# Rotation tables in one round, the opening's squares off GpSimd, the first norm ahead of block 1's split, history copies on ScalarE

## The chip, the cores and the metric

The kernel runs on one core of one Trainium2 chip. The metric is the device time of one execution in microseconds (us), the median over several runs. A core has TensorE (PE in the profile; its weight loads are PEld), VectorE (DVE), ScalarE (ACT), GpSimd (POOL) and SyncE (SP, which issues nearly all transfers here; its queue is SPq). Matmul results land in PSUM, everything else is in SBUF or in device memory (HBM).

## The reference

One hybrid decoder layer over 2048 tokens of width 1024, in float32. Cut to what matters:

```python
h = rms_norm(x, norm_in)
c_q, c_kv, k_rope, gdn_qkv, gdn_a, gdn_b, mem_q, gate = split_cols(h @ w_in, ...)
cos, sin = cos(positions * inv_freq), sin(positions * inv_freq)      # 32 frequencies
q = rms_norm(c_q) @ w_q_b;  kv = rms_norm(c_kv) @ w_kv_b             # q_rope, k_rope rotated
o_mla = causal_mla(q_nope, q_rope, k_nope, k_rope, v)                # 4 heads
qkv = silu(causal_depthwise_conv(gdn_qkv, gdn_conv))                 # 4 taps
o_gdn = rms_norm(gated_delta_rule_chunked(...))                      # 4 heads
o_mem = memory_attention(mem_q, mk, mv)                              # 4 heads, 256 memory tokens
x = x + (concat(o_mla, o_gdn, o_mem) * silu(gate)) @ w_out
y = rms_norm(x, norm_final)
```

## The kernel before

All large products are done as three matmuls of halves: an operand is split into a rounded high part and the rest (`hh` and `hl` for the activations, `wh` and `wl` for the weights), and `mm3` (line 317) adds high x high, high x low and low x high into one PSUM buffer. The tokens are worked in two halves of 1024 (`hf`), each of two blocks of 512 (`b`).

A planner runs while the program is written. It keeps a clock for every engine (`T`, line 146), charges each instruction a cost (`act_cost`, `dve_cost`, `pool_cost`, `pe_cost`, from line 204), and resumes background generators (`bg`, `spawn`, `pump`, lines 322 to 338) when the clock of PE passes their due time. It also decides by these clocks where a weight's low half is computed (`lesser`, line 618: GpSimd if its clock isn't ahead of PE's by more than a slack, otherwise VectorE). The order of writing is a priority; the framework's scheduler then orders each engine's instructions, save those that are pinned (`pin`, line 236) and keep the order in which they were written. Each engine works its queue in order.

The opening (`x_opening`, line 1911) is pinned. It loads four weight tiles and eight tiles of x^T for block 0, splits both, and runs four projections on block 0. x is not yet normed: the split takes the gain `norm_in` only (`x_split`, line 582), and the norm's factor is applied when a PSUM buffer is emptied (`scaled`, line 567, by `R[b]`). `prepare` (line 1939) splits one x tile, squares it on ScalarE and adds the square to `accs[b]`, on GpSimd or VectorE by the clocks. `behind(b)` (line 1966) makes the norm: transposes of the sum on PE (`channel_rms`, line 458), a reduction (`xss`) and some 13 small operations on VectorE (`rsqrt`), a diagonal (`dg`, in `spread`), a matmul `rb` and a copy to `rms` on ScalarE. Only then can the four PSUM buffers be emptied (`abt`, then three `gt`), and PE goes on. Block 1's x tiles are split by the same `prepare`: four of them ahead of block 0's norm, two within it, two behind it; block 1's norm is formed in the same way from its own sum of squares.

`later_rows` (line 542) makes the norms of blocks 2 and 3 in another way: it loads 128 rows of x at a time and sums the squares along the row on ScalarE (`token_sums`, line 475, does the same for given rows). `trig_tables` (line 493) computes cos and sin of all positions in the background, in two rounds of 1024 positions. Each round holds three pages of 128x1024, in which the 32 frequencies are repeated four times over the partitions; GpSimd does the product with `invf`, the rounding and the reduction by parts of 2 pi, VectorE the conversion and the clamp, ScalarE the Sin. The tables go to HBM (`trig`) and are read back by `key_rope` (line 715) and by `q_use` (line 1147). `conv_consume` (line 802) empties a PSUM buffer of the convolution's input into `raw`, copies three columns of history in and out (`hist`), multiplies the first tap on ScalarE (`y`), and adds the other three on VectorE. `token_scalars` (line 742) works out the delta rule's gates on 32 partitions (`tks`); PE transposes them (`pc`). `delta_head` (line 834) does one head of the delta rule: `kq`, `kk`, a triangular solve on GpSimd (`X`, `pr`, 62 instructions), then the scan. Attention and the output projection follow.

Of the kernel before, what the change touches and what calls it, by code (L numbers as in the profile page):

```python
# [20 lines left out]
P = 128  # L21
S = 2048
# [44 lines left out]
def hybrid_layer(ctx, tc, a, out):  # L67
# [15 lines left out]
    trig = dt("trig", [2, P, S])  # L83
# [409 lines left out]
    def trig_tables():  # L493
        parts = _pi_parts()
        magic = 1.5 * 2.0**23
        for b in range(2):
            bs = slice(b * HALF, (b + 1) * HALF)
            yield from take(page=3)
            ang, kk, tmp = (page("trig") for _ in range(3))
            pi = kk.bitcast(I32)  # L500
            dma(out=pi, in_=a["positions"][:, bs].partition_broadcast(P))
            yield 0
            V.tensor_copy(ang, pi)
            yield 0
            G.tensor_tensor(ang, ang, invf.broadcast_to([P, HALF]), op=ALU.mult)
            G.tensor_scalar(kk, ang, 1.0 / (2 * math.pi), magic, op0=ALU.mult, op1=ALU.add)
            G.tensor_scalar(kk, kk, 1.0, -magic, op0=ALU.mult, op1=ALU.add)
            yield 0
            for c in parts:
                G.tensor_scalar(tmp, kk, -c, 0.0, op0=ALU.mult, op1=ALU.add)  # L510
                G.tensor_tensor(ang, ang, tmp, op=ALU.add)
                yield 0
            V.tensor_scalar(ang, ang, -3.1415925, 3.1415925, op0=ALU.max, op1=ALU.min)
            yield 0
            A.activation(kk, ang, AF.Sin)
            A.activation(ang, ang, AF.Abs)
            A.activation(ang, ang, AF.Sin, bias=halfpi, scale=-1.0)
            yield 0
            dma(out=trig[1, :, bs], in_=kk)
            dma(out=trig[0, :, bs], in_=ang)  # L520
            yield 0
            give(page=3)
        done["trig"] = True

# [190 lines left out]
    def key_rope(hf, b):  # L715
        c0 = hf * HALF + b * 512
# [5 lines left out]
        dma(out=cs, in_=trig[0, :, c0:c0 + 512])  # L722
        dma(out=sn, in_=trig[1, :, c0:c0 + 512])
# [78 lines left out]
    def conv_consume(hf, i, y, key=None):  # L802
# [19 lines left out]
        def consume(b, ps):  # L822
# [4 lines left out]
            V.tensor_copy(raw[:, 0:3], hist[:, i, :])  # L827
            V.tensor_copy(hist[:, i, :], raw[:, 512:515])
# [318 lines left out]
    def q_use():  # L1147
# [9 lines left out]
        def use(hf, t, hs, ls, wh, wl):  # L1157
# [10 lines left out]
            for b in range(2):  # L1168
                c0 = hf * HALF + b * 512
# [741 lines left out]
    def x_opening():  # L1911
# [24 lines left out]

        accs = [t2("acc") for _ in range(2)]

        def prepare(b, k, x):

            x_split(b, k, x)
            if k == 0:
# [238 lines left out]
```

## Time and profile before

| | |
|---|---|
| median of 3 runs | 1859.41 us (1857.65 to 1865.71) |
| the profiled execution | 1856.66 us, of which the span is 1854.9 us |
| PE busy, granted clock | 1745.2 us (94% of the span), 0.978 |
| DVE, ACT, POOL busy | 1203.0 us (65%), 733.1 us (40%), 510.2 us (28%) |
| instructions | 28648 |
| transfers | 292.49 MB, mean 158 GB/s |

The profile is of one execution. Its page gives busy times by engine and in 40 slices of the span; the trace behind it gives busy times by stretch, groups of instructions, the waits of an engine with what ended them, and the instructions in order of time. A busy PE can still run at the lower of its two clock levels; the granted clock says at which it ran (1.00 is 2.4 GHz, 0.50 is 1.2 GHz).

### The profile page before, as it was taken

To read this page: it belongs to the slowest core of one execution; us is meant where nothing else is said; L and a number is where in the kernel's file an instruction comes from. 1 tells how busy PE (TensorE), PEld (TensorE's weight loads), DVE (VectorE), ACT (ScalarE), POOL (GpSimd) and SP (SyncE) were. 2 spreads that over 40 slices of the span, in tenths; PEclk is the share of its full clock that TensorE was granted. 3 is DMA by queue.
4 is the path that set the end of the run, shared out by engine and by line. 5 is a ranking of instruction groups with operands and counts; after the bars stand their busy time and mean duration, and the time that the engine had idled before them with its cause. 6 is when DMAs were issued, how large, how long until landed. Compare 5 with 4: busy or idle time off the path is not lost.

```text
span 1854.9 us, 28648 instructions
## 1 busy us (share of the span) xinstructions
PE 1745.2 (94%) x9780; PEld 1464.9 (79%) x9780; DVE 1203.0 (65%) x2696; ACT 733.1 (40%) x1792; POOL 510.2 (28%) x834
## 2 busy tenths in 40 slices
PE   6898799989998999899999799999999999899998
PEld 5676678877776888687888687889999998788886
DVE  8878586657776777546668263777776777543443
ACT  6354234334343445223454233455555556222221
POOL 5524615241161223342212524001111103511120
PEclk8899899999999999999999899999999999999999
DMA  5445347524647543455555367626252535754541
GB/s 191 156 127 153 118 154 219 183 82 136 213 131 242 160 158 121 151 195 165 181 190 192 99 208 225 183 89 185 73 173 70 157 105 176 228 168 157 184 150 61
DMA packets 242481, 292.49 MB, mean 158 GB/s; under 512 B 46848, under 2 KB 148224, under 8 KB 242336
## 3 DMA queue, kind: packets, MB, share of 16 engines
q1 hardware_dynamic: 239264, 282.28, 48.8%
q0 software_dynamic: 3072, 8.39, 1.3%
q8 instruction: 77, 1.26, 0.3%
q14 instruction: 68, 0.56, 0.1%
HBM read 197.53 MB, written 93.06 MB: 157 GB/s over the span
## 4 chain that ended last, share of the span: by engine, by line
PE 56%; DMA 6%; DVE 4%; POOL 3%; issue 2%; ACT 1%; SPq 1%; DVEq 0%; POOLq 0%; ACTq 0%
PE ip L257 14%; PE op L257 14%; PE sc L257 9%; PE av L257 6%; PE pt L257 4%; PE qb L257 2%; PE pa L257 2%; POOL X L257 1%; POOL pr L257 1%; SPq L301 1%; DMA wr<-in_w_in 1%; PE inv L257 1%; PE mv L257 1%; PE kk L257 1%; DVE y L257 1%
## 5 line engine op out<-in xcount | busy, mean ns | idle before, releaser
L257 PE MATMUL ip<-hh,wh 128*128 128x512 f32 x1088 | 457.2, 420 | 27.1 <-DVE elo L257 9.6
L257 PE MATMUL ip<-hh,wl 128*128 128x512 f32 x1088 | 433.0, 398 | 4.0 <-DVE wl L257 2.9
L257 PE MATMUL ip<-hl,wh 128*128 128x512 f32 x1088 | 432.1, 397 | 0.4 <-DVE hl L257 0.4
L257 PEld LDWEIGHTS ip<-hh,wh 128*128 128x128 f32 x1088 | 208.4, 192 | 64.5 <-DVE elo L257 10.0
L257 POOL TENSOR_TENSOR wl<-wr,wh 128x512 fp32r<-128x512 f32 x87 | 118.7, 1366 | 492.8 <-ACT wh L257 429.6
L257 PEld LDWEIGHTS ip<-hh,wl 128*128 128x128 f32 x1088 | 207.3, 191 | 50.4 <-DVE wl L257 3.6
L257 PEld LDWEIGHTS ip<-hl,wh 128*128 128x128 f32 x1088 | 208.8, 192 | 35.8 <-DVE hl L257 1.3
L257 PE MATMUL op<-wop,mh 128*128 128x512 f32 x480 | 151.2, 396 | 6.5 <-ACT mh L257 6.5
L257 ACT CAST wh<-wr 128x512 fp32r<-128x512 f32 x146 | 90.1, 618 | 157.8 <-PE ip L257 86.0
L257 DVE TENSOR_TENSOR tl<-pt,th 128x512 fp32r<-128x512 f32 (+2 forms) x208 | 119.8, 585 | 32.6 <-ACT th L257 30.3
L257 PE MATMUL sc<-kn,qn 128*128 128x512 f32 (+2 forms) x480 | 133.6, 380 | 0.0
L257 PE MATMUL av<-th,vn 128*128 128x256 f32 x576 | 130.3, 287 | 2.0 <-ACT th L257 2.0
L257 DVE SCALAR_TENSOR_TENSOR y<-raw,gdn_conv,y 128x512 f32<-128x512 f32 x144 | 125.4, 878 | 7.7 <-ACT y L257 6.3
L257 ACT CAST th<-pt 128x512 fp32r<-128x512 f32 (+2 forms) x158 | 80.1, 513 | 103.7 <-PE pt L257 96.5
L257 POOL TENSOR_TENSOR pr<-X,lt 128x60 f32<-128x60 f32 (+24 forms) x248 | 93.1, 376 | 97.6 <-DMA lt<-lsys 76.2
L257 PEld LDWEIGHTS op<-wop,mh 128*128 128x128 f32 x480 | 90.7, 190 | 27.0 <-ACT mh L257 7.0
L257 PEld LDWEIGHTS av<-th,vn 128*128 128x128 f32 x576 | 98.5, 189 | 6.9 <-ACT th L257 2.1
L257 POOL TENSOR_TENSOR X<-X,pr 128x60 f32<-128x60 f32 (+24 forms) x248 | 94.0, 379 | 19.4
L257 PE MATMUL sc<-kr,qr 128*128 128x512 f32 (+2 forms) x320 | 97.3, 381 | 0.0
L290 POOL DMA_DIRECT2D mix<-mo x64 | 34.8, 545 | 221.7 <-ACT mo L257 193.5
L257 PE MATMUL op<-wop,ml 128*128 128x512 f32 x240 | 94.5, 394 | 0.0
L257 POOL TENSOR_TENSOR og<-og,orow 128x512 f32<-128x512 f32 x32 | 45.9, 1451 | 172.5 <-DMA orow<-ri 130.4
(282 smaller groups left out, 3547.3 us busy)
## 6 DMA issues: line engine op xcount, KB each, us to landing
wr<-in_w_in SPq DMA_DIRECT2D x148, 256.0 KB, 2.9
fr<-rows_n SPq DMA_DIRECT2D x48, 256.0 KB, 4.4
mxo<-mix SPq DMA_DIRECT2D x16, 768.0 KB, 5.1
craw<-craw SPq DMA_DIRECT2D x40, 256.0 KB, 3.1
x<-in_xT SPq DMA_DIRECT2D x32, 256.0 KB, 5.3
gatem<-gt SPq DMA_DIRECT2D x32, 256.0 KB, 2.2
qn<-qn SPq DMA_DIRECT2D x32, 256.0 KB, 3.1
kn<-kn SPq DMA_DIRECT2D x32, 256.0 KB, 3.6
```

What stands on the lines that cost most here:

```text
L257: return pinned(f(*args, **kw))
L290: pinned(nc.gpsimd.dma_start(out=raw(out), in_=raw(in_)))
L301: ins = pinned(nc.sync.dma_start(out=raw(out), in_=raw(in_)))
```

## The change

The tables `trig` are laid out as four chunks of 32 frequencies by 512 positions, so that one round of 128x512 holds all positions; two pages are taken instead of three, and the readers repeat the 32 rows over the heads while they load (`trig_load`). In the opening only block 0 has a sum of squares, and its adds are always on VectorE. All of block 1's splits are written behind block 0's norm diagonal (four) and behind the norm row (four). Block 1's norm comes from four loads of 128 rows of x, squared and summed on ScalarE. The two history copies of `conv_consume` go from VectorE to ScalarE.

```diff
@@ -80,7 +80,7 @@
     def dt(name, shape, dtype=F32):
         return dram.tile(list(shape), dtype, name=name, tag=name)
-    trig = dt("trig", [2, P, S])
+    trig = dt("trig", [2, 4, 32, 512])
     ab = dt("ab", [2, 8, HALF])
     rows_g = dt("rows_g", [2, 32 * P])
     rows_l = dt("rows_l", [2, 32])
@@ -491,36 +491,42 @@
         return acc
     def trig_tables():
         parts = _pi_parts()
         magic = 1.5 * 2.0**23
-        for b in range(2):
-            bs = slice(b * HALF, (b + 1) * HALF)
-            yield from take(page=3)
-            ang, kk, tmp = (page("trig") for _ in range(3))
-            pi = kk.bitcast(I32)
-            dma(out=pi, in_=a["positions"][:, bs].partition_broadcast(P))
-            yield 0
-            V.tensor_copy(ang, pi)
-            yield 0
-            G.tensor_tensor(ang, ang, invf.broadcast_to([P, HALF]), op=ALU.mult)
-            G.tensor_scalar(kk, ang, 1.0 / (2 * math.pi), magic, op0=ALU.mult, op1=ALU.add)
-            G.tensor_scalar(kk, kk, 1.0, -magic, op0=ALU.mult, op1=ALU.add)
-            yield 0
-            for c in parts:
-                G.tensor_scalar(tmp, kk, -c, 0.0, op0=ALU.mult, op1=ALU.add)
-                G.tensor_tensor(ang, ang, tmp, op=ALU.add)
-                yield 0
-            V.tensor_scalar(ang, ang, -3.1415925, 3.1415925, op0=ALU.max, op1=ALU.min)
-            yield 0
-            A.activation(kk, ang, AF.Sin)
-            A.activation(ang, ang, AF.Abs)
-            A.activation(ang, ang, AF.Sin, bias=halfpi, scale=-1.0)
-            yield 0
-            dma(out=trig[1, :, bs], in_=kk)
-            dma(out=trig[0, :, bs], in_=ang)
-            yield 0
-            give(page=3)
+        yield from take(page=2)
+        pg, pt = page("trig"), page("trig")
+        ang, kk, tmp = pg[:, 0:512], pg[:, 512:1024], pt[:, 0:512]
+        pi = kk.bitcast(I32)
+        for c in range(4):
+            dma(out=pi[c * 32:(c + 1) * 32], in_=a["positions"][:, c * 512:(c + 1) * 512].partition_broadcast(32))
+        yield 0
+        V.tensor_copy(ang, pi)
+        yield 0
+        G.tensor_tensor(ang, ang, invf.broadcast_to([P, 512]), op=ALU.mult)
+        G.tensor_scalar(kk, ang, 1.0 / (2 * math.pi), magic, op0=ALU.mult, op1=ALU.add)
+        G.tensor_scalar(kk, kk, 1.0, -magic, op0=ALU.mult, op1=ALU.add)
+        yield 0
+        for c in parts:
+            G.tensor_scalar(tmp, kk, -c, 0.0, op0=ALU.mult, op1=ALU.add)
+            G.tensor_tensor(ang, ang, tmp, op=ALU.add)
+            yield 0
+        V.tensor_scalar(ang, ang, -3.1415925, 3.1415925, op0=ALU.max, op1=ALU.min)
+        yield 0
+        A.activation(kk, ang, AF.Sin)
+        A.activation(ang, ang, AF.Abs)
+        A.activation(ang, ang, AF.Sin, bias=halfpi, scale=-1.0)
+        yield 0
+        for i, t in ((1, kk), (0, ang)):
+            dma(out=trig[i].rearrange("c f t -> (c f) t"), in_=t)
+        yield 0
+        give(page=2)
         done["trig"] = True
+    def trig_load(t, i, c, n):
+        dma(out=t[0:n * 32],
+            in_=trig[i, c].unsqueeze(0).broadcast_to([n, 32, 512]))
     def evac_split(ps, dst, n=512):
@@ -713,14 +719,13 @@
         return consume
     def key_rope(hf, b):
-        c0 = hf * HALF + b * 512
         while "trig" not in done:
             yield POLL
         yield from take(t2=3)
         kr, cs, sn = t2("kr"), t2("cs"), t2("sn")
         dma(out=kr[0:64], in_=krr_d[hf * 2 + b])
-        dma(out=cs, in_=trig[0, :, c0:c0 + 512])
-        dma(out=sn, in_=trig[1, :, c0:c0 + 512])
+        trig_load(cs, 0, hf * 2 + b, 2)
+        trig_load(sn, 1, hf * 2 + b, 2)
         yield 0
         tA, tB = t2("ra"), t2("rb")
         V.tensor_tensor(tA[0:32], kr[0:32], cs[0:32], op=ALU.mult)
@@ -824,8 +829,8 @@
                 y.append(page("y"))
             raw = x2("raw", (P, 515))
             whole(hf, b, raw[:, 3:515], ps)
-            V.tensor_copy(raw[:, 0:3], hist[:, i, :])
-            V.tensor_copy(hist[:, i, :], raw[:, 512:515])
+            A.copy(raw[:, 0:3], hist[:, i, :])
+            A.copy(hist[:, i, :], raw[:, 512:515])
             yb = y[0][:, b * 512:(b + 1) * 512]
             A.activation(yb, ps if hf else raw[:, 3:515], AF.Copy, scale=taps[:, i, 3:4])
             spawn(rest(b, raw, yb))
@@ -1166,11 +1171,10 @@
                     yield POLL
                 return
             for b in range(2):
-                c0 = hf * HALF + b * 512
                 yield from take(t2=3)
                 cs, sn = t2("cs"), t2("sn")
-                dma(out=cs, in_=trig[0, :, c0:c0 + 512])
-                dma(out=sn, in_=trig[1, :, c0:c0 + 512])
+                trig_load(cs, 0, hf * 2 + b, 4)
+                trig_load(sn, 1, hf * 2 + b, 4)
                 yield 0
                 r1, r2 = project(b, hs, ls, *half), project(b, hs, ls, wh, wl)
                 tA, tB, tC = t2("ra"), t2("rb"), t2("rc")
@@ -1934,49 +1938,55 @@
             lesser("wl").tensor_tensor(wl, w, wh, op=ALU.subtract)
             return wh, wl
-        accs = [t2("acc") for _ in range(2)]
-        def prepare(b, k, x):
-            x_split(b, k, x)
+        acc = t2("acc")
+        def prepare(k, x):
+            x_split(0, k, x)
             if k == 0:
-                A.activation(accs[b], x, AF.Square)
+                A.activation(acc, x, AF.Square)
                 return
             sq = t2("sq")
             A.activation(sq, x, AF.Square)
-            (G if T["POOL"] <= T["DVE"] + 600 else V).tensor_tensor(accs[b], accs[b], sq, op=ALU.add)
+            V.tensor_tensor(acc, acc, sq, op=ALU.add)
         H[:] = ([], [], []), ([], [], [])
         ws = [[], []]
         for i in range(FIRST):
             ws[0].append(split(wp[i][:, 0:512], "m2", "m2"))
             if i == 0:
-                prepare(0, 0, xs[0])
+                prepare(0, xs[0])
         for k in range(1, KT):
-            prepare(0, k, xs[k])
+            prepare(k, xs[k])
             xs1.append(x_load(1, k - 1))
             if k == KT // 2:
                 ws[1] = [split(w[:, 512:1024], *(("wh", "wl") if i < 3 else ("m2", "m2"))) for i, w in enumerate(wp)]
         xs1.append(x_load(1, KT - 1))
+        grab(page=4)
+        rows = [page("xrow") for _ in range(4)]
+        for j, t in enumerate(rows):
+            dma(out=t, in_=a["x"][(4 + j) * P:(5 + j) * P, :], first=True)
         for t, src in deferred:
             if t is not g_in:
                 dma(out=t, in_=src, awaited=False)
-        for k in range(KT // 2):
-            prepare(1, k, xs1[k])
         def behind(b):
-            step_end[0] = ready(accs[b])
-            yield 0
-            parts = yield from channel_rms(accs[b], D)
+            if b == 0:
+                step_end[0] = ready(acc)
+                yield 0
+                parts = yield from channel_rms(acc, D)
+            else:
+                parts = inverse_rms((yield from token_sums(rows, 4)), D)
+                give(page=4)
             row = rms_row(b, parts)
             next(row)
             if b == 0:
-                for k in (4, 5):
-                    prepare(1, k, xs1[k])
+                for k in range(4):
+                    x_split(1, k, xs1[k])
             yield EARLY
             yield from row
             if b == 0:
-                for k in (6, 7):
-                    prepare(1, k, xs1[k])
+                for k in range(4, KT):
+                    x_split(1, k, xs1[k])
                 give(A=1, x2=CONV)
                 done["block1"] = True
             else:
```

## Rows read from the trace of the kernel before

**Rows 1.** The page: busy time by engine; PE's granted clock in 40 slices, in tenths.
```profile
PE 1745.2 (94%) x9780; PEld 1464.9 (79%) x9780; DVE 1203.0 (65%) x2696; ACT 733.1 (40%) x1792; POOL 510.2 (28%) x834
...
PEclk8899899999999999999999899999999999999999
```

**Rows 2.** Busy us by stretch: from:to and length, each engine, PE clock, DMA share.
```profile
24.00:46.00 22.00, 14.72 (x56) 10.90 (x55) 21.53 (x33) 10.96 (x19) 12.32 (x9) 0.78 0.18 47
...
77.00:92.00 15.00, 7.96 (x25) 5.96 (x24) 14.90 (x21) 2.83 (x6) 14.32 (x9) 0.66 0.26 81
...
125.00:165.00 40.00, 33.13 (x137) 26.46 (x136) 38.83 (x48) 9.14 (x15) 24.22 (x14) 0.96 0.38 109
...
250.00:1030.00 780.00, 747.45 (x4069) 614.68 (x4068) 529.76 (x1099) 304.15 (x792) 234.06 (x419) 0.99 0.53 168
```

**Rows 3.** PE in time order (start, length, [idle before]); PE's waits, 0 to 180 us.
```profile
37.50 1.40 PE L257 MATMUL rb<-dg,ones 128*128 128x512 f32 x2 [3.83 <-DVE dg L257]
41.98 0.77 PE L257 MATMUL ip<-hh,wh 128*128 128x512 f32 x1 [3.09 <-DVE abt L257]
...
PE pc L257 <- DVE tks L257: 7.0, 3, 4.2
...
PE kk L257 <- DVE kq L257: 4.0, 2, 2.1
...
PE ip L257 <- DVE wl L257: 2.9, 1, 2.9
```

**Rows 4.** Busy us by stretch, columns as in rows 2: behind the first norm's waits.
```profile
40.00:44.00 4.00, 2.02 (x5) 1.66 (x6) 4.00 (x6) 2.73 (x6) 3.12 (x2) 0.50 0.57 165
```

**Rows 5.** Groups of DVE (10 to 32) and POOL (10 to 46); DVE in time order.
```profile
L257 DVE SCALAR_TENSOR_TENSOR hl<-x,norm_in,hh 128x512 fp32r<-128x512 f32 x11 | 14.4, 1362 | 0.5 <-ACT hh L257 0.4
...
L257 POOL TENSOR_TENSOR acc<-acc,sq 128x512 f32<-128x512 f32 x14 | 21.7, 1548 | 13.8 <-ACT sq L257 13.1
...
8.51 0.75 DVE L257 SCALAR_TENSOR_TENSOR hl<-x,norm_in,hh 128x512 fp32r<-128x512 f32 x1 [6.44 <-ACT hh L257]
...
31.93 0.68 DVE L257 TENSOR_REDUCE xss<-sq 128x4 f32<-128x512 f32 x1
...
36.76 1.29 DVE L257 TENSOR_TENSOR dg<-ident,rc 128x512 fp32r<-128x512 f32 x2
37.97 1.41 DVE L257 SCALAR_TENSOR_TENSOR hl<-x,norm_in,hh 128x512 fp32r<-128x512 f32 x2
```

**Rows 6.** The tile trig: its POOL instructions (ns min/median/max, first and last start).
```profile
L257 POOL TENSOR_SCALAR trig<-trig x12: 1044/1368/2449, 72.6 to 150.8; 128x1024 f32<-128x1024 f32 x12
L257 POOL TENSOR_TENSOR trig<-trig x8: 2337/2382/2844, 78.7 to 152.2; 128x1024 f32<-128x1024 f32 x8
```

**Rows 7.** POOL and DVE in time order, one overlap.
```profile
82.34 2.34 POOL L257 TENSOR_TENSOR trig<-trig 128x1024 f32<-128x1024 f32 x1
...
82.51 2.19 DVE L257 TENSOR_TENSOR rc<-rc 128x4 fp32r<-128x4 f32 x1
```

**Rows 8.** Groups of DVE: 125 to 165 us, then 260 to 1170 us.
```profile
L257 DVE SCALAR_TENSOR_TENSOR y<-raw,gdn_conv,y 128x512 f32<-128x512 f32 x12 | 18.2, 1543 | 0.0
...
L257 DVE SCALAR_TENSOR_TENSOR y<-raw,gdn_conv,y 128x512 f32<-128x512 f32 x106 | 84.2, 801 | 2.6 <-ACT y L257 1.4
```

**Rows 9.** The tile hist (ns min/median/max); a short ACT instruction in time order.
```profile
L257 DVE COPY raw<-hist x48: 149/163/2310, 75.2 to 1070.2; 128x3 f32<-128x3 f32 x48
...
67.85 0.18 ACT L257 ACTIVATE ea<-gdn_a_log 32x1 f32<-32x1 f32 x1
```

**Rows 10.** Busy us by stretch, columns as in rows 2, GB/s last: the opening's loads.
```profile
10.00:24.00 14.00, 14.00 (x59) 11.44 (x58) 13.55 (x13) 13.20 (x23) 10.58 (x7) 1.00 1.04 395
```

**Rows 11.** PE's waits, 1030 to 1060 us; busy us just behind them.
```profile
PE ip L257 <- DVE elo L257: 9.6, 1, 9.6
PE mk L257 <- DVE gt L257: 2.0, 1, 2.0
...
1048.00:1056.00 8.00, 5.26 (x18) 4.25 (x19) 3.88 (x18) 4.65 (x21) 2.52 (x2) 0.50 0.53 171
```

## The prediction

> **What bounds the kernel now.** I read the page first: TensorE is busy 94% of the span and its granted clock is near full in most slices [rows 1]. So a microsecond is won only where TensorE stands idle, or runs at the lower of its two clock levels. The second view, busy time by stretch, says where that is [rows 2]. From 250 to 1030 us TensorE is busy 747.5 of 780 us at clock 0.99. The opening is worse: it loses 7.3 of 22 us at 24 to 46, 7.0 of 15 at 77 to 92, and 6.9 of 40 at 125 to 165, and in each of these stretches VectorE is busy almost without a break (21.5 of 22, 14.9 of 15, 38.8 of 40). The third view, TensorE's waits, names VectorE at all of them: the diagonal of the first norm (3.83 us), the first evacuation `abt` (3.09), the token scalars (7.0 in three), `kq` (4.0 in two), a weight residue `wl` (2.9) [rows 3]. After such a gap the clock is at half, that is 1.2 instead of 2.4 GHz: 0.50 at 40 to 44 us [rows 4]. The mean clocks of rows 2 price this: 14.7 busy us at 0.78 lose 3.2, 8.0 at 0.66 lose 2.7, 33.1 at 0.96 lose 1.3.
>
> **Why VectorE is late there.** The same instruction has two prices. The low half `hl` takes 1.41 us for two when GpSimd is idle, but 1362 ns each, eleven times, while GpSimd adds squares (`acc`, 14 adds of 1548 ns) [rows 5]. The convolution step `y` takes 1543 ns at 125 to 165 us, beside the second round of rotation tables, and 801 ns later on [rows 8]. One pair shows how: GpSimd's add on `trig` starts at 82.34 and runs 2.34 us; VectorE's operation on 128x4 elements starts at 82.51 and takes 2.19, so that both end together [rows 7]. Such VectorE instructions stand still until GpSimd's ends. The change takes away exactly the GpSimd work in these three stretches.
>
> **Part 1, the opening (24 to 46 us).** Removed: all 14 adds on GpSimd, and block 1's eight squares. Seven adds for block 0 move to VectorE; at the price of a residue or `hl`, 0.7 us, they are 4.9 us. Four `hl` of block 1 that stood ahead of the norm move behind it. VectorE's queue ahead of the norm is then 8 `hl`, 7 `wl` and 7 adds, 22 x 0.7 = 15.4 us; the first `hl` starts at about 8.5 us, so the sum of squares is ready at 24. Transposes 0.6, then from the reduction to the diagonal what it takes now (31.93 to 36.76, 4.8 us), then the diagonal 1.3: 30.7 instead of 38.05 [rows 5]. Behind it, in program order, come all eight `hl` of block 1 (5.6 us) and only then `abt` (0.7): TensorE gets its first free PSUM buffer at about 37 instead of 41.98. Block 0's matmuls keep TensorE busy to 33.67 as now (37.50 less 3.83, rows 3). That is 4.9 us, and about a third of the 3.2 of clock: **6 us**. Bounds: 3, if the `hl` wait for ScalarE one by one and one or two `wl` also come ahead of `abt`; 10, if both gaps and the clock loss go.
> Block 1's norm now takes four row loads of 512 KB and four squares with accumulation on ScalarE. The loads join SP's queue ahead of the small constants, 2.1 MB, 5.3 us at the 395 GB/s that the DMA engines gave at 10 to 24 us [rows 10]; the DMA engines are 18% busy at 24 to 46 [rows 2], which hides them. Without that cover the next weight loads would come 5 us late. ScalarE is half idle in that stretch and loses eight squares for the four. TensorE has four PSUM buffers to fill before it needs block 1's norm, so I cost this at nothing.
>
> **Part 2, the tables.** Before, two rounds of 128x1024 on GpSimd: 12 tensor_scalar (median 1368 ns) and 8 adds (2382 ns), 35 us [rows 6], and two products with `invf`. The new layout holds all 2048 positions in one round of 128x512: 11 instructions, half as many at half the length, some 10 us. The first round lies over the token scalars now and will again, because it is started at the same place in the job order. So their wait doesn't go; VectorE is held by pieces half as long and a round half as long. I take 4 of the 7.0 + 2.7 us [rows 2, 3]. Bounds: 0 (the pieces fall as badly) and 9.7 (the round slips past the scalars).
> The second round goes altogether. At 125 to 165 us, 12 `y` lose 0.74 us each (1543 less 801), 9 us of VectorE's 38.8, without the small copies [rows 8]. The three waits there, 6.9 us, and 1.3 of clock stand behind that queue: **6 us**, bounds 2.5 (only the `wl` wait goes; `kq` then waits for its factor rows) and 8.2.
> Off the path: half the Sin work and two of four table switches on ScalarE, two pages held instead of three, once instead of twice, and two more position issues on SP.
> The tables are read back through a source repeated over heads. What the trace shows: the waits of TensorE in rows 3 and 11 are none of them put down to these loads. The Trainium skill, "DMA: Bandwidth & Descriptors", section "Rules for kernel authors", speaks against this form: an outermost dimension of fewer than 16, such as a leading zero-stride broadcast, confines a transfer to at most that many of the 16 engines. By that rule a 256 KB load of four copies would move in 2.7 us instead of 0.7 (an estimate from that page and the 395 GB/s of rows 10).
>
> **Part 3, history copies.** 96 copies of 128x3 leave VectorE, where one takes 163 ns but up to 2310 beside GpSimd, and join ScalarE, where an activation on 32x1 takes 0.18 us [rows 9]: 17 us over the whole kernel on an engine that is 40% busy [rows 1]. The new wait is ScalarE's for the evacuation `raw`; queued behind it are `y`'s first product, which waits for `raw` today, and the weight casts `wh`. I take 0, bounds +2 (casts 0.4 us later, some of them felt) and -2.
>
> **The sum.** 6 + 4 + 6 = 16 us off the profiled execution's 1856.66 us (span 1854.9): 1840.7. That execution lies 2.75 us under the median of the runs shown, 1859.41, so the forecast is 1859.4 - 16 = **1843**. From 250 us on I carry the gain unchanged, since TensorE is the bound. The program's own planner lays out every later instruction anew, though, and its gaps will fall otherwise: 32 us of idle at 250 to 1030. I allow 6 us either way.
>
> **Rivals.**
> *The gain is taken up by what comes next.* With VectorE free, `abt`, the scalars and `kq` wait for the next thing in line: ScalarE's `hh`, the first half-length round, the factor rows. For: all three lower bounds are such cases. Against: VectorE's queue has no gap in these stretches. The lower bounds add up to 5.5: 1854.
> *The repeated source slows the rope.* For the page's rule named above, against it nothing here but that these loads end no wait of TensorE. As a mechanism: four pairs of query-rope products hold two PSUM buffers each until sin and cos have landed; 2 us later for each, with nothing to hide it, is 8 us: 1851.
> *Slower: a weight residue behind a solve.* At 1039 us TensorE waits 9.6 and 2.0 us and then runs 5.3 busy us at 0.50, 2.6 lost, 14.2 in all [rows 11]. There GpSimd is in one of the eight triangular solves, and the low half of a memory weight has been put behind it. The planner chooses GpSimd or VectorE by its own clock of GpSimd, and the change alters that clock from the first microsecond (14 adds and half the tables gone), so it will call GpSimd free more often. One such collision more eats the gain (1857); from two on the kernel is slower: 1843 + 28 = 1871. Against: there is one in the present trace, with seven other solves that have none.
> *All of it goes.* The three upper bounds, 10 + 9.7 + 8.2 = 28: 1831.
>
> **How the numbers follow.** Forecast 0.55, all of it 0.13, taken up 0.15, the rope 0.05, the collisions 0.12. About 0.5% (9.3 us) is what a measurement of this kernel can tell from no change. Faster: forecast and all of it, 0.68. Within 0.5%: 0.20. Slower: 0.12. The range starts 6 us of re-planning below the upper bounds' 1831, less the third of that case that I leave out, at 1826; at the top it takes in the taken-up case with the 6 us of re-planning, 1860, and leaves the collisions out.
>
> **What would show it.** Right: 11 GpSimd instructions on the tables with some 10 us in all and none after 100 us; `hl` in the opening near 0.75 us; the waits before the diagonal and `abt` together under 4; the scalars' wait near 3; `y` near 0.8 at 125 to 165 with no wait on `kq` or `wl` above 1 us. Wrong: the opening's waits unchanged with ScalarE or a DMA named; a wait on a residue beside a solve; or three quiet stretches up to 165 us, with the same total, so that the gain is lost further on.

## The result and the profile after

The changed kernel takes 1877.17 us (median, 1873.02 to 1885.85), the kernel before 1860.53 in the same rounds: ratio 1.0093, 95% interval 1.0067 to 1.0119. It is 17 us slower; the forecast was 1843, 16 us below the 1859.4 it started from. Its profiled execution took 1876.02 us (span 1874.2), 19.4 more than the one of before.

The three stretches of rows 2 first, busy time by stretch, and one further on (columns: span; busy us and instructions of PE, PEld, DVE, ACT, POOL; granted clock; DMA share; GB/s):

```profile
24.00:46.00 22.00, 19.46 (x81) 15.66 (x80) 17.87 (x44) 14.71 (x28) 4.96 (x5) 0.92 0.78 259
77.00:92.00 15.00, 14.65 (x66) 11.77 (x66) 11.37 (x25) 7.24 (x15) 6.72 (x6) 1.00 0.37 122
125.00:165.00 40.00, 33.94 (x141) 27.35 (x141) 35.61 (x62) 10.35 (x20) 7.41 (x5) 0.91 0.50 152
250.00:1030.00 780.00, 723.27 (x3926) 590.41 (x3926) 490.17 (x987) 295.15 (x817) 221.19 (x398) 0.98 0.51 160
```

The opening and the scalars are better than in rows 2 (19.46 busy us for 14.7, 14.65 for 8.0). The fourth row is the surprise: 723.3 busy us where before had 747.5. TensorE's waits of after, at 24 to 46 us, 46 to 125 (one line) and 125 to 165 (one line):

```profile
PE ip L257 <- DVE abt L257: 2.5, 1, 2.5
...
PE pc L257 <- DVE tks L257: 1.3, 2, 1.1
...
PE ip L257 <- DVE wl L257: 4.9, 1, 4.9
```

The diagonal's 3.83 us are gone, `abt`'s 3.09 are 2.5, the scalars' 7.0 are 1.3 [rows 3]. `kq` ends no wait at 125 to 165 any more, and a `wl` ends one of 4.9. What VectorE and GpSimd do there (groups: count, min/median/max ns, first and last start):

```profile
L257 POOL TENSOR_SCALAR trig<-trig x6: 615/622/957, 67.3 to 84.2; 128x512 f32<-128x512 f32 x6
L257 POOL TENSOR_TENSOR trig<-trig x4: 1291/1608/1679, 73.6 to 85.2; 128x512 f32<-128x512 f32 x4
...
L257 DVE SCALAR_TENSOR_TENSOR hl<-x,norm_in,hh x16: 733/744/1784, 8.5 to 37.8; 128x512 fp32r<-128x512 f32 x16
...
L257 DVE SCALAR_TENSOR_TENSOR y<-raw,gdn_conv,y x8: 735/745/1165, 125.9 to 149.2; 128x512 f32<-128x512 f32 x8
```

One round of tables, 11.7 us in all with the product by `invf` and done by 87 us; `hl` at 744 ns where eleven took 1362 [rows 5]; `y` at 745 [rows 8]. All much as forecast. Now the whole span in two windows, before and then after:

```profile
0.00:250.00 250.00, 206.21 (x938) 163.39 (x939) 195.24 (x365) 105.91 (x219) 118.62 (x127) 0.93 0.47 150
250.00:1200.00 950.00, 902.58 (x5118) 746.79 (x5117) 616.80 (x1325) 361.11 (x950) 287.39 (x547) 0.98 0.54 170
```

```profile
0.00:250.00 250.00, 217.29 (x1002) 172.96 (x1003) 172.58 (x357) 106.32 (x250) 75.35 (x110) 0.97 0.53 163
250.00:1200.00 950.00, 875.84 (x4916) 718.71 (x4916) 575.67 (x1185) 352.05 (x980) 286.36 (x549) 0.97 0.53 163
```

Busy time by clock is work done. A window's clock is a mean that takes in idle time too, so over eight shorter stretches, those named here and what lies between: 209.5 full-speed us by 250 us against 194.5, 15 ahead. In the next 950 us TensorE is idle 74.2 us against 47.4. Two landmarks place the loss: the first state product `pa` and the first attention score `sc` (the first start is the first number after the durations), before and then after:

```profile
L257 PE MATMUL pa<-st,y x128: 270/275/582, 271.5 to 1208.6; 128*128 128x128 f32 x128
L257 PE MATMUL sc<-kn,qn x480: 276/393/507, 1156.8 to 1550.6; 128*128 128x512 f32 x112, 128*128 128x256 f32 x32, 128*128 128x384 f32 x16
```

```profile
L257 PE MATMUL pa<-st,y x128: 270/275/377, 262.8 to 1227.4; 128*128 128x128 f32 x128
L257 PE MATMUL sc<-kn,qn x480: 274/393/487, 1175.9 to 1569.1; 128*128 128x512 f32 x112, 128*128 128x256 f32 x32, 128*128 128x384 f32 x16
```

After is 8.7 us ahead at `pa` and 19.1 behind at `sc`: 27.8 us are lost in between, and nothing behind. TensorE's longest waits at 250 to 1100 us in after:

```profile
PE pa L257 <- DVE r L257: 12.2, 2, 11.3
PE rb L257 <- DVE dg L257: 9.7, 2, 9.3
PE rn L257 <- DVE fac L257: 9.1, 3, 7.4
PE mk L257 <- ACT bwh L257: 7.9, 1, 7.9
PE oT L257 <- DVE y L257: 7.5, 2, 6.5
```

None of these five is a long wait of before. Here is the second of them, in order of time, on SyncE's queue, then GpSimd, VectorE and TensorE (start, duration; in brackets the idle time before and what ended it):

```profile
479.67 0.33 SPq L301 DMA_DIRECT2D wr<-in_w_in  x1
492.73 2.52 SPq L301 DMA_DIRECT2D tsys<-X  x4
495.35 0.54 SPq L301 DMA_DIRECT2D mq<-ehi  x1
495.99 0.39 SPq L301 DMA_DIRECT2D mq<-mq  x1
...
492.49 0.21 POOL L257 TENSOR_TENSOR X<-X,pr 128x8 f32<-128x8 f32 x1
...
487.28 0.78 DVE L257 TENSOR_TENSOR dg<-ident,rc 128x512 fp32r<-128x512 f32 x1
497.68 0.69 DVE L257 TENSOR_TENSOR dg<-ident,rc 128x512 fp32r<-128x512 f32 x1 [9.63 <-issue]
...
498.43 0.80 PE L257 MATMUL rb<-dg,ones 128*128 128x512 f32 x1 [9.29 <-DVE dg L257]
```

`tsys<-X` are the stores of a triangular solve, and GpSimd ends that solve at 492.7. SyncE has stood at them since 480 and issues nothing, though the copies of `mq` behind them need nothing of the solve. They are issued right after the stores, and only then does VectorE write its second `dg`, a buffer from the same ring as `ehi`, and the norm of the memory query goes on. That `dg` waits for this buffer follows from the order of these starts; the trace puts no name to it ("issue"). SyncE's waits for `X` at 0 to 1200 us (us in total, times, longest), before and after:

```profile
SPq L301 <- POOL X L257: 38.8, 4, 14.6
```

```profile
SPq L301 <- POOL X L257: 77.9, 6, 18.7
```

The last of the five waits stands behind the new table loads. VectorE's waits for table loads at 0 to 1200 us, before (one line) and then after; behind those of after the stretch in order of time on VectorE and TensorE:

```profile
DVE rb L257 <- DMA sn<-trig: 0.9, 1, 0.9
```

```profile
DVE rb L257 <- DMA sn<-trig: 9.6, 6, 3.5
DVE ra L257 <- DMA cs<-trig: 8.2, 2, 6.2
...
630.52 0.68 DVE L257 TENSOR_TENSOR ra<-kr,cs 32x512 f32<-32x512 f32 x1 [6.18 <-DMA cs<-trig]
...
633.39 0.68 DVE L257 TENSOR_TENSOR rb<-kr,sn 32x512 f32<-32x512 f32 x1 [2.11 <-DMA sn<-trig]
...
655.54 0.67 DVE L257 TENSOR_TENSOR y<-y,inv_ro 128x512 f32<-128x512 f32 x1
...
656.27 1.11 PE L257 MATMUL oT<-ident,y 128*128 128x128 f32 x4 [6.49 <-DVE y L257]
```

From 624 us to this `y` VectorE is never idle but for these two waits and a third, 1.10 us at 649, also for `sn`. So VectorE's queue came to the `y` 9.4 us late, and TensorE waited 6.49 for it. That the loads were slower, and not only later, is shown in the section on why the prediction was wrong.

### The profile page after: what moved, and what is told of

It reads as the page before. It is cut to its first block, busy times and chain, and to the rows that moved or that the text cites. A ratio compares the mean times of both kernels' runs of the same rounds, so it can differ in the third digit from the quotient of the medians.

```text
span 1874.2 us, 28621 instructions
## 1 busy us (share of the span) xinstructions
PE 1749.7 (93%) x9776; PEld 1464.7 (78%) x9776; DVE 1153.0 (62%) x2590; ACT 734.3 (39%) x1884; POOL 467.9 (25%) x822
## 5 line engine op out<-in xcount | busy, mean ns | idle before, releaser
L257 POOL TENSOR_TENSOR wl<-wr,wh 128x512 fp32r<-128x512 f32 x100 | 137.4, 1375 | 602.8 <-ACT wh L257 490.3
L257 PEld LDWEIGHTS ip<-hl,wh 128*128 128x128 f32 x1088 | 209.1, 192 | 35.2 <-DVE hl L257 0.5
L257 DVE SCALAR_TENSOR_TENSOR y<-raw,gdn_conv,y 128x512 f32<-128x512 f32 x144 | 116.1, 810 | 27.0 <-ACT y L257 25.4
L257 POOL TENSOR_TENSOR pr<-X,lt 128x60 f32<-128x60 f32 (+24 forms) x248 | 87.0, 351 | 81.3 <-DMA lt<-lsys 48.0
L257 POOL TENSOR_TENSOR X<-X,pr 128x60 f32<-128x60 f32 (+24 forms) x248 | 90.2, 364 | 19.4
L257 ACT ACTIVATE s<-s,m 128x768 f32<-128x768 f32 (+13 forms) x71 | 79.1, 1115 | 31.4 <-DVE mx L257 30.1
```

Source lines behind the costliest of these rows:

```text
L257: return pinned(f(*args, **kw))
```

## Experiments

All numbers in one table, for the sections below. "Price" is the planner's for a small GpSimd step, explained with those runs. PE busy and clock are those at 250 to 1200 us; the last column is SyncE's wait for `X` at 0 to 1200 us (in brackets, where SyncE has no such store, its wait for those stores to land).

| run | median us | ratio (95%) | PE busy, clock | SP waits for X |
|---|---|---|---|---|
| before | 1858 to 1861 | 1 | 902.6, 0.98 | 38.8 |
| after | 1877.2 | 1.0093 (1.0067, 1.0119) | 875.8, 0.97 | 77.9 |
| e1 tables alone | 1897.6 | 1.0196 (1.0169, 1.0223) | 872.4, 0.96 | 43.1 |
| e2 opening alone | 1878.4 | 1.0091 (1.0076, 1.0106) | 880.5, 0.97 | 51.7 |
| e3 history alone | 1866.4 | 1.0032 (1.0017, 1.0047) | 903.4, 0.97 | 15.5 |
| e4 after, stores on GpSimd | 1868.3 | 1.0047 (1.0032, 1.0061) | 888.5, 0.97 | (70.2) |
| e5 tables, plan held | 1873.7 | 1.0064 (1.0043, 1.0085) | 890.3, 0.97 | 34.9 |
| e6 before, neutral | 1863.8 | 1.0017 (1.0006, 1.0028) | 898.5, 0.98 | 40.3 |
| e7 after, neutral | 1874.9 | 1.0074 (1.0046, 1.0102) | 882.0, 0.97 | 61.2 |
| e8 before, stores on GpSimd | 1876.9 | 1.0086 (1.0052, 1.0120) | 888.5, 0.97 | (72.6) |
| e9 copies, plan held | 1864.7 | 1.0035 (1.0015, 1.0055) | 901.5, 0.98 | 41.6 |
| e10 copies' plan, old work | 1864.1 | 1.0031 (1.0014, 1.0048) | 900.8, 0.98 | 16.1 |
| e11 after, price +110 | 1848.6 | 0.9945 (0.9923, 0.9968) | 899.0, 0.98 | 33.2 |
| e12 after, stores and loads on GpSimd | 1870.1 | 1.0070 (1.0049, 1.0091) | 887.1, 0.97 | (67.5) |
| e13 before, price +110 | 1876.9 | 1.0095 (1.0076, 1.0114) | 891.5, 0.97 | 67.0 |
| e14 after, +110, neutral | 1848.5 | 0.9943 (0.9920, 0.9965) | 892.7, 0.98 | 28.1 |
| e15 after, price +160 | 1835.0 | 0.9871 (0.9843, 0.9900) | 914.8, 0.98 | 14.4 |
| e16 opening, price +110 | 1865.4 | 1.0023 (1.0009, 1.0038) | 898.8, 0.97 | 75.9 |
| e17 before, price +160 | 1831.1 | 0.9853 (0.9828, 0.9879) | 919.1, 0.99 | 11.9 |
| e18 after, price +220 | 1839.9 | 0.9899 (0.9871, 0.9926) | 903.7, 0.98 | 32.5 |

**The three parts alone (e1, e2, e3).** Each is the kernel before with one part of the diff: the table round and its readers; the opening; the two `A.copy` lines.

> The kernel before with the tables alone changed (one round of 128x512, loads repeated over the heads). My theory, that the work of the change is as cheap as forecast and that the loss comes from where the newly planned order puts SyncE's waits for the triangular solves: by 200 us TensorE is 8 to 12 us ahead of the kernel before, and the total is decided by how long SyncE stands at the stores of the solves (tsys<-X, 36 us before, 77 us after), so 1845 to 1875 in step with that number. Rival, that a part costs its time by itself: if the tables are that part (their loads on few DMA engines, their pages), about 1875 with waits of TensorE on the rope's products; if not, about 1850.

> The kernel before with the opening alone changed (adds on VectorE, block 1's norm from rows of x, norm ahead of block 1's split). My theory: 5 to 7 us ahead by 60 us, as in the kernel after, and a total that follows SyncE's time at the solves' stores. Rival: if the four row loads or the later split cost the time by themselves, about 1875 and a loss that is already there at 200 us.

> The kernel before with the history copies alone on ScalarE. My theory: the 96 copies cost ScalarE some 17 us off the path; TensorE no earlier at 60 us and 3 to 6 us earlier at 165 us; the total follows SyncE's time at the solves' stores. Rival: if ScalarE's queue makes the convolution late, about 1870 with waits on y spread over every head.

Alone they cost 36, 17 and 6 us (ratio less 1, times 1860); together 17, not 59. So no sum of parts explains the result: what a part costs depends on the plan that it falls into. Nor does the total go with SyncE's standing at the stores, as was expected: e1 stands 43.1 us there and takes 1897.6, e3 stands 15.5 and takes 1866.4. The opening alone does what was forecast early, its first `pa` starts at 261.7 us against 271.5, and is 17 us late at the end.

**Small edits that keep the work (e6, e7).** `LAT`, the planner's signal time, is 160 for 150, in before and in after.

> The kernel before with one number of the planner altered, the latency it adds to a step (LAT 150 to 160 ns), and no work changed. Theory, that the time of this kernel hangs on where the plan happens to put its waits and that the kernel before is a favourable one: it moves by 5 us or more, to 1866 to 1895, with other waits of TensorE above 3 us than before. Rival, that the plan is stable and a part of the change costs its time by itself: within 5 us of 1861.

> The kernel after with the same neutral number (LAT 150 to 160 ns), no work changed. Theory: it moves by 5 us or more either way from 1877 while its first 200 us stay 10 us or more ahead of the kernel before. Rival: within 5 us of 1877, with the waits at 311, 489, 757 and 1061 us in their places.

Three us up, two down, so the theory's 5 us or more did not come. A moved order need not cost anything either: under the higher price (e14, below) the same edit moves 408 of SyncE's instructions, and the time stays within 0.2 us of e11's.

**The plan held (e5, e9, e10).** In e5 the new tables are computed, while the clocks are charged with the two old rounds; in e9 the copies run on ScalarE and VectorE's clock is charged; e10 is the reverse, old work under the order that the copies' change makes:

```diff
-        V.tensor_copy(raw[:, 0:3], hist[:, i, :])
+        note("DVE", dve_cost("tensor_copy", (o, x), {}, o), [o], [x])   # e10: note("ACT", act_cost(...))
+        pinned(nc.scalar.copy(o, x))                                    # e10: nc.vector.tensor_copy(o, x)
```

> The tables of e1 (one round of 128x512, read back over the heads) with the planner's clocks charged as if the two old rounds were still there, so that the program is written in the order of the kernel before; the second round is charged and not issued. Theory, that the new layout of the order and not the tables' own work costs the time: 30 us or more faster than e1's 1897, at 1848 to 1865, with TensorE ahead of the kernel before at 200 us. Rival, that the tables' loads or their shape cost it: within 8 us of 1897.

> The history copies run on ScalarE, and the planner's clocks are charged as if they ran on VectorE, so that nearly the order of before is kept (11 of SyncE's and 153 of VectorE's instructions out of place, against 327 and 1273 with the copies charged where they run, which took 1866.4 us, +5.9). Theory (the order, not the work, costs the time): 1860 us, ratio 0.998 to 1.002. Rival (the copies load ScalarE and delay the casts): 1866, as with the free order.

> The reverse of the run beside it: the history copies stay on VectorE, as in before, and the planner's clocks are charged as if ScalarE did them, so that the work is that of before and the order that of the history change alone (328 of SyncE's and 1231 of VectorE's instructions out of place). Theory (the order costs the time): 1866 us, +5 to +7 on before, with the wait of some 10 us near 552 us that the history change alone had. Rival (the work costs it): 1860, as before.

Holding the plan gives the tables back 24 of their 36 us: that much of their loss goes with the order, and neither expectation for e5 fits. Twelve stay, and they are not the order's: in the two traces TensorE works the same 9780 matmuls, by their names, in the same order. e5 is 6 us ahead of before at 222 us, 4 ahead at 590, 4 behind at 630 and 13 behind at the end. The stretch in between, with a cast on ScalarE and a wait of TensorE in it, before and then e5:

```profile
590.00:640.00 50.00, 47.86 (x243) 38.86 (x242) 33.66 (x59) 16.77 (x36) 9.65 (x7) 1.00 0.54 171
...
600.92 0.62 ACT L257 CAST wh<-wr 128x512 fp32r<-128x512 f32 x1 [1.71 <-DMA wr<-in_w_in]
...
601.75 0.49 PE L257 MATMUL pa<-vn,kt 128*128 128x128 f32 x2 [0.77 <-ACT vn L257]
```

```profile
590.00:640.00 50.00, 41.79 (x196) 34.47 (x196) 25.70 (x47) 12.81 (x30) 6.85 (x5) 0.90 0.47 139
...
600.87 0.62 ACT L259 CAST wh<-wr 128x512 fp32r<-128x512 f32 x1 [5.43 <-DMA wr<-in_w_in]
...
601.70 0.63 PE L259 MATMUL pa<-vn,kt 128*128 128x128 f32 x2 [4.49 <-ACT vn L259]
```

In both, the weight load `wr` is issued right behind a load of `cs` and one of `sn`. Before casts it 5.9 us after its issue at 595.05, e5 9.1 us after its issue at 591.77. `vn` stands behind that cast in ScalarE's queue, and TensorE waits for `vn`. At 623 us VectorE then waits 4.01 us for `sn` (0.95 in before), and TensorE 3.55 for the `r` behind it (0.83). With the granted clock at 0.90 in this stretch, against 1.00, e5 does 37.6 full-speed us in it where before does 47.9. So at this place the new loads cost the time with the order unchanged; the rest of e5's loss isn't followed up here. For the copies the pair decides nothing: the work under nearly the old order and the old work under the new order both cost some 6 us, as both together do. e10 did bring back the wait before `inv` near 550 us (12.2 us at 547.5) without a single copy moved, so that wait is the order's.

**The solves' stores moved off SyncE's queue (e4, e8, e12).** The stores of the solves are issued by GpSimd instead of SyncE, in after and in before; in e12 the reloads `inv<-tsys` too.

```diff
-        ins = pinned(nc.sync.dma_start(out=raw(out), in_=raw(in_)))
+        q = nc.gpsimd if out.tensor.name[:4] == 'tsys' else nc.sync     # e12: or in_.tensor.name[:4] == 'tsys'
+        ins = pinned(q.dma_start(out=raw(out), in_=raw(in_)))
```

> The kernel after with the four stores of each solve (tsys<-X) issued by GpSimd, which has just made X, and nothing else changed; the planner's clocks are charged as before. My theory: SyncE no longer stands 77 us at these stores, TensorE's waits of 11.3 us at 311, 9.3 at 489 and 7.9 at 1061 go or shrink to under 3 each, and the total falls by 15 to 30 us, to 1847 to 1862. Rival, that a part costs its time by itself: SyncE's standing is a symptom, the total stays within 5 us of 1877.

> The kernel before with the stores of the solves issued by GpSimd, the control to e4. Theory that SyncE's standing at these stores is what costs the time: SyncE stands 36 us there before, so it gains a few us (TensorE's 6.7 at 222 goes), to 1850 to 1858. Rival, that e4's 9 us came from another draw of the order: no gain, 1858 to 1870.

> The changed kernel with both the solves' stores and their reloads issued on GpSimd's queue, so that SyncE's queue is never held by a solve. Theory (SyncE's queue standing is what the change lost): the waits of 11.3 us at 311 and 7.4 at 757 us go too, and with the 9 us that the stores alone gave the kernel takes 1850 to 1862 us. Rival (GpSimd now stands at the reloads, which wait for the stores to land, and the next solve or weight residue waits for that): no better than with the stores alone, 1866 to 1878.

In after the stores alone give 9 us back, and the wait at 489 us goes. In before the same edit costs 16. But in none of the three is SyncE relieved. It stands until the stores have landed, at the reload or at the next solve's load of the identity into `X`. Its waits in e4 and then in e8:

```profile
SPq L302 <- DMA tsys<-X: 70.2, 9, 20.1
```

```profile
SPq L302 <- DMA tsys<-X: 72.6, 10, 21.7
```

So e4 holds the queue about as long as after does (77.9), and e8 longer than before (38.8). With the reloads moved too, after is at 1870, no better than e4: the waits of 11 us before `r` and 8 before `fac` stay, and SyncE stands 68.6 us, five times, at the identity's load. What a queue that no solve holds would be worth is thus untested. That this standing is the whole loss is refuted by e3, with 15.5 us of it and no gain, and by e1. It isn't SyncE's longest wait either: for residues `wl` made on GpSimd it stands 136.4 us in before and 185.2 in after, and no run takes that away.

**The planner's price (e11, e13 to e18).** The planner charges a GpSimd tensor_tensor 147 ns plus 2.1 per element, and 102 ns between two that depend on each other. A solve has 62 such steps of 50 elements on the mean, so the planner ends it after 22.0 us. In the trace of before the eight solves last 23 to 33 us, 28.2 on the mean. A higher price for the 44 steps of up to 64 elements makes the planner's solve 26.8 us (110 ns more), 29.0 (160) and 31.7 (220); so 160 is the nearest to the trace of before, where the expectations below still put 110. After's own eight solves last 26.9 us on the mean, nearest to 110.

```diff
-            return 147 + 2.1 * free(out)
+            return 147 + 2.1 * free(out) + (110 if free(out) <= 64 else 0)   # e15, e17: 160; e18: 220
```

> The changed kernel, in which only the planner's price of a small GpSimd tensor_tensor is raised by 110 ns (free size up to 64), to what the solves in the traces take. It computes the same with the same work; 385 of SyncE's instructions are emitted in another place. Theory (the planner thinks each solve done some 7 us early and puts its stores, its reload and VectorE's work behind it too early in the in-order queues): SyncE stands less at the solves' stores than 76.8 us and the kernel takes 1855 to 1866 us. Rival (any new order is a fresh draw, and a better price buys nothing by itself): 1865 to 1885, with other large waits in other places.

> The kernel before with the same higher price for a small GpSimd tensor_tensor (110 ns more). If the 28 us that this price gave the changed kernel are the change's own gain set free, this kernel stays at 1852 to 1865 us and the change is worth 5 to 15 us under the better price. If the price alone is the gain, this kernel reaches 1840 to 1850 and the change is worth nothing under it. If each new order is a fresh draw, it goes up, to 1865 to 1880, since the kernel before had a good one.

> The changed kernel with the higher price, and the planner's signal time 160 ns for 150: the work is the same, 408 of SyncE's and 642 of VectorE's instructions stand elsewhere than with the higher price alone. Theory (the better price works in whatever order it makes): 1845 to 1858 us. Rival (one lucky order): 1862 to 1885, like the changed kernel's other orders so far (1868 to 1877).

> The changed kernel with 160 instead of 110 ns added to the price of a small GpSimd tensor_tensor; 295 of SyncE's and 715 of VectorE's instructions stand elsewhere than with 110. The planner's solve is then about 3 us longer than the traces'. Theory (better too late than too early in a queue that runs in order): 1845 to 1858 us, few SyncE stands at the solves' stores. Rival (a lucky order at 110): 1862 to 1885.

> The opening alone, with the higher price. With the old price it took 1878.4 us, 17 over before, though it was 6 us ahead at 64 us. Theory (the loss lies in the solves' places in the queues): 1850 to 1862 us. Rival (fresh draws): anywhere from 1855 to 1885, with no more likelihood of the lower end.

> The kernel before with 160 ns more for a small GpSimd tensor_tensor. If the gain of the same edit in the changed kernel (1835.0 us) is the change's own, this stays at 1855 to 1880 us, as it did with 110 ns (1876.9). If it belongs to the price, this goes to 1840 to 1850, and the change is worth at most 10 us under it.

> The changed kernel with 220 ns more, some 4 us over what a solve takes beyond the last step. Theory (later places in the in-order queues cost little, earlier ones much): 1832 to 1852 us, with SyncE standing less than 35 us at the solves' stores. Rival (160 was a lucky draw): 1855 to 1880.

With the same operations after falls from 1877 to 1848.6, 1848.5, 1835.0 and 1839.9 us in four orders, so it is not one lucky order. A plan is more than an order, though: the price also decides which engine makes a residue. Of 148 `wl<-wr,wh` 100 are on GpSimd in after, 87 in before, and 87, 91, 91 and 84 in these four. This is the forecast gain, and more: another plan of the same operations takes back the whole loss behind 250 us. e15's two windows:

```profile
0.00:250.00 250.00, 220.73 (x1014) 176.73 (x1015) 177.39 (x363) 107.29 (x251) 74.52 (x108) 0.97 0.54 166
250.00:1200.00 950.00, 914.83 (x5184) 755.13 (x5183) 599.82 (x1287) 377.83 (x1042) 287.80 (x546) 0.98 0.54 167
```

TensorE idles 35.2 us at 250 to 1200 where after idles 74.2, and SyncE stands 14.4 us at the stores instead of 77.9. But before gains by the price as well: with 160 ns it takes 1831.1, the best of all. With 110, which is nearer to its solves than the old price, it loses 17, so a truer price doesn't by itself make a better plan. Its windows at 160:

```profile
0.00:250.00 250.00, 214.10 (x989) 171.60 (x990) 207.78 (x389) 110.04 (x226) 120.17 (x127) 0.96 0.48 153
250.00:1200.00 950.00, 919.05 (x5246) 760.07 (x5245) 625.38 (x1374) 371.67 (x985) 283.14 (x544) 0.99 0.55 173
```

At one and the same price the change is thus worth +17 us (old price), +11 (old price, signal time 160), -28 (110) and +4 (160), the last within the noise of the two runs. Under 160 the changed kernel has done 213.3 full-speed us by 250 us, over the same shorter stretches, against 207.4. It gives these 5.9 back and more where the second half of the tokens begins. Three stretches there, e15 and then e17:

```profile
530.00:550.00 20.00, 16.45 (x83) 13.04 (x82) 14.15 (x28) 5.47 (x11) 5.92 (x2) 0.83 0.68 226
550.00:570.00 20.00, 16.41 (x62) 12.53 (x61) 9.33 (x16) 4.69 (x9) 2.56 (x2) 0.83 0.43 120
610.00:630.00 20.00, 14.56 (x66) 11.68 (x65) 19.68 (x52) 8.66 (x30) 4.95 (x3) 0.94 0.41 122
```

```profile
530.00:550.00 20.00, 18.17 (x85) 14.49 (x85) 6.85 (x11) 3.26 (x7) 3.44 (x7) 1.00 0.72 233
550.00:570.00 20.00, 17.98 (x148) 13.86 (x148) 17.74 (x24) 9.92 (x19) 5.87 (x5) 0.91 0.70 225
610.00:630.00 20.00, 18.69 (x92) 15.42 (x91) 18.30 (x35) 11.17 (x30) 4.07 (x3) 1.00 0.39 128
```

e15 does 41.0 full-speed us (busy time by clock) in these three, e17 53.2. What ends TensorE's waits at 520 to 650 us in e15 is two residues `wl` on GpSimd (4.7 us) and the scalars of the second half (4.5 for `nt`), work that the change doesn't touch, and a cast `wh` (2.7). That cast stood 3.45 us at a weight load issued at 549.24, right behind a load of `sn` at 548.56.

What stays open: the change's own worth. Before's work took 1831 to 1877 us in the orders tried, the changed work 1835 to 1877; the two ranges lie on each other, and no run puts both into one order. No run leaves the repeated source out of the change and keeps the rest, either. The versions that beat both kernels are e17 and e15.

## Why the prediction was wrong

Point by point, by its steps.

*What bounds the kernel, and why VectorE is late in the opening*: right. With GpSimd's adds and second round gone, `hl` and `y` fell to the price that the forecast gave them (0.744 and 0.745 us).

*Part 1*: forecast 6 us. At 24 to 46 us the work done rose from 11.5 (14.7 at 0.78) to 17.9 (19.46 at 0.92): 6.4. Behind `abt` TensorE went on at 36.0 against the forecast's 37, though for another reason than said: four of block 1's eight `hl` stood ahead of it and not all eight, but one of the four took 1.78 us and a residue came between.

*Part 2, scalars*: forecast 4. The wait fell from 7.0 to 1.3. At 60 to 92 us, a window that takes in the scalars' earlier place, the work done rose from 22.3 to 28.1 (13.40 and 14.65 at clock 1.00): 5.8. *Second round*: forecast 6. At 125 to 165 us the work done fell by 0.9 (33.13 at 0.96, 33.94 at 0.91), since a `wl` took over the wait (ahead of it VectorE had stood 3.2 us at a `kr` load that was issued behind a table load); at 165 to 250 it rose by 6.9 (72.39 at 0.94, 78.04 at 0.96). Together 6.0. Another wait between, on `y` before `sq`, took 3.7 at 92 to 125. All stretches up to 250 us add up to 15 against the forecast 16.

*The repeated source*: put at nothing in the sum and left to a rival at 0.05: **this step failed too.** That table loads end no wait of TensorE in the kernel before says nothing of loads of another form. From issue to the last completion in the trace the 16 table loads take 3.4 to 5.7 us in before, 4.6 in the median, and 5.5 to 11.9 in after, 8.1 in the median. In the trace's semaphore records a load of before ends with 16 completions, one of after with as many as its source has copies, 2 or 4. The Trainium skill, "DMA: Bandwidth & Descriptors", section "Rules for kernel authors", would have such a load confined to as many of the 16 engines as it has copies; the trace agrees.

The rival had the query-rope products wait for these loads, 8 us in all, and none of TensorE's waits names them. What waited was VectorE, 17.8 us in after against 0.9 in before, and TensorE behind it: 6.5 us before `oT` in after. Where a weight load came behind a table load, ScalarE waited, and TensorE behind that: 4.5 us before `vn` in e5. The whole price of the loads in after stays open.

*History copies*: forecast 0, bounds +-2. A copy on ScalarE takes 190 ns, 96 of them 18 us, as forecast; alone the edit costs 6 us, and the runs don't tell work from order there.

*"From 250 us on I carry the gain unchanged, since TensorE is the bound"*, with "6 us either way" for the new plan: **this step failed.** TensorE is the bound of that stretch on the mean, but 47 of its 950 us are idle, and the plan moves that figure: in the twenty versions of the table TensorE's busy time there runs from 872 us (e1, 1897.6 us in all) to 919 (e17, 1831.1). The term for re-planning was mis-sized: not 6 us but some 20 either way, as the runs of before's own operations show (1831.1 in e17, 1876.9 in e13). The prediction had seen that every later instruction is laid out anew; it then priced that by the idle time present, as if it could only fall elsewhere, not grow. Of the four other plans of before's operations that were tried (e6, e10, e13, e17) three are slower than it, so a new draw may have been more likely to lose; four are too few to say. Of the signs that the prediction named, quiet stretches with the gain lost further on is the one that came.

*The rival on the slower side* had the right place and, as far as TensorE's waits tell, the wrong mechanism. The planner did call GpSimd free more often, as it said (100 residues `wl` there for 87). But `wl` on GpSimd ends only 2.0 us of TensorE's waits at 250 to 1100 us in after. The solves did harm through SyncE's queue and through VectorE's order behind it, in part: the waits before `dg` and `bwh` stand behind the stores, and moving the stores returned 9 of the 17 us in after, but took 16 in before. Why one plan of the same operations is 20 us longer than another isn't reduced to one cause here, and no run separates its order from the engine of its residues.

## What to carry to other kernels

When a planner lays out the whole program by its own clocks, an edit at the front is two edits: the work it saves, and a new order of everything behind it. Cost the second by running the old work in a few other orders, for that spread (here some 20 us either way) is the real width of the forecast; a single before and after cannot tell a gain that is smaller than it. Before judging such an edit, compare the planner's durations with the trace: one price of a dependent chain, here the solve's (22 us against 28), moved the time by as much as the edit did or more, down in five of the six runs that raised it on the whole of before or after, though up by 17 us in the other.

An edit that changes the form of a transfer wants a price for it even where the old form cost nothing. The price may be paid elsewhere: by the instruction that stands behind its reader in an in-order queue, or by the next load.

## What the runs showed of the hardware

- A transfer that waits for another engine holds everything behind it in SyncE's queue: 12.6 us at 480 us in after, with copies behind it that needed nothing of the solve. Moving that transfer to another queue let SyncE stand at the next dependent ones (70.2 us in e4, 67.5 in e12).
- A chain of small GpSimd operations is slower than its parts: the median step of a solve takes 0.30 us (201 to 886 ns in after), while its eight solves of 62 steps last 26.9 us on the mean, 0.43 a step with the gaps and a residue put between.
- A load whose source is repeated 2 or 4 times in its outermost dimension ended with 2 or 4 completions instead of 16 and landed 8.1 us after its issue against 4.6 for the plain one (medians of 16, after and before). Its issue took SyncE longer too, 562 ns against 424 for `cs` (medians of eight).
- Such a load held up the weight load issued behind it: 9.1 us from issue to cast in e5, 5.9 in before, with the same instructions around it.
